# Neighbourhood attention: scores in three shared banks, division on the outputs, smaller weight buffers

## The chip, the cores and the metric

The kernel runs on one core of one Trainium2 chip. The metric is the device time of one execution in microseconds, taken as the median of several runs; lower is better. The profile comes from one further execution. The engines are TensorE (PE in the profile; PEld is its weight load), VectorE (DVE), ScalarE (ACT), GpSimd (POOL) and SyncE (SP), which issues nearly all DMAs of this kernel.

## The reference, cut to what matters

Two layers of a diffusion block work on 1024 latent tokens (a grid of 16 rows by 64 columns) and 256 context tokens, 1024 wide. Each layer modulates and normalises the tokens, multiplies them by one wide input matrix, gives its columns to four mixers (linear attention, neighbourhood attention, a state-space model, pooling), gates the four results, multiplies by an output matrix, normalises and adds. The neighbourhood attention, per head (4 heads of 64):

```
s_win = q @ k_rows + bias        # a window of 8 rows x 16 columns around the query; -inf outside
s_ctx = q @ k_context            # all 256 context tokens
p = softmax(concat([s_win, s_ctx], axis=-1), axis=-1)
o = p[window] @ v_rows + p[context] @ v_context
```

Context tokens attend to context tokens alone, without a bias. In the second layer they are no queries any more.

## The kernel before, in words

Every product that needs full accuracy is split: each operand is held as a rounded high half and a low half (float32r), and three products (high by high, high by low, low by high) are summed. `load_w` (L289) brings a weight matrix in pieces of `per` blocks of 128 rows: a raw piece by DMA, its high half by a cast on ScalarE (L301), its low half by a subtraction (L302). The pool `wp` has two raw buffers and three for each half (`WB`, L66), all as large as the largest piece: 1152 numbers, 4.5 KB a partition. Only the first projection of each layer, in `gla_proj` (L828), is 288 columns wide; the others are 128, 256 or 512 wide.

Attention (`na`, L1229) goes over jobs: a head and a block `qb` of 128 queries. Blocks 0 and 1 are the context (layer 0 only), blocks 2 to 9 cover 8 grid columns each. So a layer has 4 x 10 or 4 x 8 jobs, in rising order. An inner block meets 3 blocks of window keys and 2 of context (640 scores a query), the edge blocks 2 and 9 meet 2 and 2 (512), a context block 2 (256).

- `na_head` (L1267) loads what a head needs: the bias table of 1408 columns (one buffer; the inner table, the left and the right edge table, with zero columns for the context), negated on ScalarE (L1272), K (two buffers), Q in two tiles for blocks 0 to 4 and 5 to 9 (two buffers in all), V (one buffer). From block 6 on the next head's loads are asked for; those whose buffer is still in use wait on SyncE's queue.
- `na_scores` (L1291) multiplies Q by K into the tile `nS` (two banks of PSUM, one buffer), adds the bias on VectorE and takes the extreme of each row (L1321), forms the exponential and its row sum on ScalarE (L1326), takes the reciprocal (L1328) and multiplies the 640 probabilities by it (L1329).
- `na_turn` and `na_rest` turn the probabilities on TensorE (L1359) into `nT` tiles (one bank each, three buffers) three jobs later, and split them in halves (L1365 on ScalarE, L1366 on VectorE).
- `na_values` (L1369), two jobs later still, multiplies them by V for a pair of jobs (L1381), into the right half of the `nT` tile that `na_rest` used; ScalarE copies the lower partitions (L1383), VectorE adds the two parts into the head's output (L1395).

Pooling work on GpSimd and the first loads of the output stage (`out_early`) are woven in between. Beside the attention of layer 0, TensorE does five of the eight gate projections (`proj_gates`, L317), which have a later priority; in layer 1 they are done by 1155 us. The order on each engine's queue is fixed when the program is built: a planner takes the instructions by priority and by its own estimate of when each is ready. Every engine runs its queue in that order, SyncE its DMA issues too.

Of the kernel before, what the change touches and what calls it, by code (L numbers as in the profile page):

```python
# [12 lines left out]
F32 = mybir.dt.float32  # L13
F32R = mybir.dt.float32r
I32 = mybir.dt.int32
# [25 lines left out]
NRM = 0  # L41
# [19 lines left out]
NB = (1, 3)  # L61
# [9 lines left out]
class Kernel:  # L71
# [72 lines left out]
    def load_consts(self):  # L144
# [8 lines left out]
        self.sel = ld("sel", [128, 2])  # L153
        self.bmod = [c.tile([128, 24], F32, name=f"bmod{l}") for l in range(DEPTH)]
# [134 lines left out]
    def load_w(self, src, n, pool=(None, None), scale=None, engines=None, order=None):  # L289

        nc = self.nc
        per = min(8, 1152 // n)
        his, los = {}, {}
        for k0 in order or range(0, 8, per):
            hi, lo = (next(own, None) if own else None for own in pool)
            hi, lo = (w or self.t([128, per, n], "w" + x, b, self.wp, dtype=F32R) for w, x, b in zip((hi, lo), "hl", WB))
            raw = self.t([128, per, n], "w", WB[2], self.wp)
            (self.q(3) if order else self.q(4)).dma_start(raw, src[k0 * 128:(k0 + per) * 128, :].rearrange("(k p) f -> p k f", p=128))
# [677 lines left out]
    def gla(self, l, last):  # L976
# [6 lines left out]
        flag = self.const.tile([1, 1], I32, name=f"gflag{l}")  # L983
# [244 lines left out]

    def na(self, l, last):  # L1229


        with self.phase("na", True):
            pool = self.pooling(l, last)
            jobs = [(h, qb) for h in range(4) for qb in range(2 if last else 0, NT)]
# [6 lines left out]
            for i in range(len(jobs) + NALAG + 2):  # L1241
# [16 lines left out]
                if i < len(jobs):  # L1258
                    self.na_scores(l, live[i], last)
                if i == len(jobs) + OE:  # L1260
                    self.out_early(l, last)
# [5 lines left out]
    def na_head(self, l, h, last):  # L1267
        nc = self.nc
        rows = slice(64 * h, 64 * h + 64)
        bias = self.t([128, 1408], "nab", 1)  # L1270
        nc.sync.dma_start(bias, self.a["na_bias"][l, h])
        nc.scalar.activation(bias, bias, AF.Copy, scale=-1.0)  # L1272
# [16 lines left out]
        return h, K, Q, V, bias, self.na_y  # L1289

    def na_scores(self, l, job, last):  # L1291
# [3 lines left out]
        (h, K, Q, V, bias, yst), qb = job  # L1295
# [16 lines left out]
        for c, b, n in runs:  # L1312
            for i in range(2):
                nc.tensor.matmul(ps[:, c * 128:(c + n) * 128], lhsT=Qb[:, i, :], rhs=K[:, b * 128:(b + n) * 128],  # L1314
                                 start=(i == 0), stop=(i == 1))
        ps = ps[:, off * 128:off * 128 + nk]
# [3 lines left out]
        if blocks:  # L1320
            v.tensor_tensor_reduce(P[:, 0:nk], ps, bias[:, b0:b0 + nk], 1.0, -NEG, ALU.add, ALU.min, nm)  # L1321
# [30 lines left out]
    def na_psum(self, tag, n):  # L1352
        return self.ps2.tile([128, n], F32, tag=tag, bufs=NB[tag == "nT"], name=self.nm(tag))

# [14 lines left out]
    def na_values(self, l, job0, job1, last):  # L1369
        nc = self.nc  # L1370
        (h, K, Q, V, bias, yst), qb, r0, _, _, shared, PT, rest, ps = job0
# [39 lines left out]
    def pooling(self, l, last):  # L1411
# [3 lines left out]
        sc = self.t([128, 2], "psc", 1)  # L1415
        nc.sync.dma_start(sc, a["pool_sc"][l])
        wb = self.t([128, 2, 128], "pwb", 1)
# [307 lines left out]
```

## Time and profile before

| what | value |
|---|---|
| timed runs | 1373.57, 1375.45, 1379.98 us; median 1375.45 us |
| profiled execution | 1365.45 us; span of its instructions 1363.6 us |
| TensorE busy | 1244.4 us (91%), 7086 products |
| VectorE busy | 909.1 us (67%) |
| ScalarE busy | 584.0 us (43%) |
| GpSimd busy | 202.0 us (15%) |
| mean granted TensorE clock | 0.976 |
| attention of layer 0 | about 494 to 617 us of the span |
| attention of layer 1 | about 1155 to 1266 us |

A busy time counts an engine's instructions where they overlap once. TensorE's products are pipelined, so a run of them is shorter than the sum of their durations. A pause is put down to the instruction that ended it.

### The profile page before, as it was taken

The numbers are of one execution on the slowest core, as the hardware profiler recorded it, in microseconds if no ns is written. First come the engines' busy times: TensorE is split into PE (matmuls) and PEld (weight loads), VectorE is DVE, ScalarE is ACT, GpSimd is POOL, SyncE is SP. The second block draws the span as 40 slices with busy tenths as digits, with TensorE's granted clock in tenths as the row PEclk, the third lists the DMA queues.
The fourth block names the chain that finished last, engine by engine and source line by source line (L and its number), as shares of the span: only waits on it lengthen the run. The fifth ranks groups of instructions, "written<-read, shape, count | busy, mean of one in ns | idle before, by whom it ended". The sixth has DMA issues, their size and how long they took to land. (4 is left out here: it accounts for less than half of the span.)

```text
span 1363.6 us, 20304 instructions
## 1 busy us (share of the span) xinstructions
PE 1244.4 (91%) x7086; PEld 1001.4 (73%) x7086; DVE 909.1 (67%) x2269; ACT 584.0 (43%) x1218; POOL 202.0 (15%) x212
## 2 busy tenths in 40 slices
PE   5799999999999999979999999999999999777897
PEld 2698967677777688867778989768767776666676
DVE  2878587555387648873866788586644884786483
ACT  2652443223333347653555643443323333665321
POOL 0100000001100024351410000000111100235220
PEclk9898999999999999989999999999999999898999
DMA  9546596752533277747832475865216435764762
GB/s 320 183 132 215 196 261 175 229 158 78 167 122 122 72 198 196 221 138 220 257 111 93 126 226 193 256 187 157 85 53 197 160 108 163 204 168 127 209 205 88
DMA packets 231542, 231.08 MB, mean 169 GB/s; under 512 B 46888, under 2 KB 192808, under 8 KB 231104
## 3 DMA queue, kind: packets, MB, share of 16 engines
q1 hardware_dynamic: 229840, 227.14, 54.8%
q10 hardware_dynamic: 1584, 2.49, 0.5%
q8 instruction: 59, 0.97, 0.3%
q14 instruction: 59, 0.48, 0.1%
HBM read 159.97 MB, written 69.62 MB: 168 GB/s over the span
## 5 line engine op out<-in xcount | busy, mean ns | idle before, releaser
L317 PE MATMUL pa<-ahi,wh 128*128 128x512 f32 (+1 forms) x664 | 171.5, 386 | 3.7 <-DVE stg L346 1.5
L317 PE MATMUL pa<-ahi,wl 128*128 128x512 f32 (+1 forms) x664 | 167.2, 379 | 0.2 <-PEq L1554 0.2
L317 PE MATMUL pa<-alo,wh 128*128 128x512 f32 (+1 forms) x664 | 164.3, 377 | 0.4 <-PEq L1554 0.4
L317 PEld LDWEIGHTS pa<-ahi,wh 128*128 128x128 f32 x664 | 115.6, 192 | 29.0 <-issue 6.0
L317 PEld LDWEIGHTS pa<-alo,wh 128*128 128x128 f32 x664 | 116.0, 192 | 22.9 <-issue 4.8
L317 PEld LDWEIGHTS pa<-ahi,wl 128*128 128x128 f32 x664 | 115.5, 192 | 23.0 <-issue 5.6
L302 POOL TENSOR_TENSOR wl<-w,wh 128x1024 fp32r<-128x1024 f32 (+1 forms) x19 | 46.9, 2470 | 286.0 <-PE pa L317 153.2
L387 PE MATMUL po<-wx,ahi 128*128 128x512 f32 x312 | 79.9, 396 | 4.3 <-ACT ahi L379 2.5
L333 PE MATMUL pa<-wh,ahi 128*128 128x256 f32 (+1 forms) x480 | 78.4, 297 | 4.9 <-DVE ahi L260 2.3
L301 ACT CAST wh<-w 128x1024 fp32r<-128x1024 f32 (+1 forms) x51 | 53.8, 1056 | 59.1 <-PE pa L317 37.5
L333 PE MATMUL pa<-wl,ahi 128*128 128x256 f32 (+1 forms) x480 | 78.2, 296 | 0.1
L333 PE MATMUL pa<-wh,alo 128*128 128x256 f32 (+1 forms) x480 | 76.1, 293 | 0.0
L1314 PE MATMUL nS<-naK,naQ 128*128 128x256 f32 (+2 forms) x256 | 58.7, 348 | 17.4 <-DVE nast L1321 16.0
L333 PEld LDWEIGHTS pa<-wh,ahi 128*128 128x128 f32 x480 | 65.6, 191 | 10.0 <-issue 3.0
L387 PEld LDWEIGHTS po<-wx,ahi 128*128 128x128 f32 x312 | 59.2, 191 | 18.0 <-ACT ahi L379 3.5
L333 PEld LDWEIGHTS pa<-wl,ahi 128*128 128x128 f32 x480 | 66.4, 192 | 3.6 <-issue 2.5
L333 PEld LDWEIGHTS pa<-wh,alo 128*128 128x128 f32 x480 | 65.0, 190 | 3.3 <-issue 2.9
L1314 PEld LDWEIGHTS nS<-naK,naQ 128*128 128x128 f32 x256 | 43.5, 199 | 30.7 <-DVE nast L1321 26.0
L1321 DVE CUSTOM_DVE_ANT_0 naP<-nS,nab 128x640 f32<-128x640 f32 (+1 forms) x64 | 50.4, 787 | 17.6 <-ACT nab L1272 9.0
L1326 ACT ACTIVATE naP<-naP,nast 128x640 f32<-128x640 f32 (+1 forms) x64 | 51.6, 806 | 24.0 <-DVE nast L1321 21.2
L1381 PE MATMUL nT<-naPT,naV 128*128 128x256 f32 (+3 forms) x368 | 54.0, 286 | 7.4 <-DVE naPT L1366 5.4
L302 DVE TENSOR_TENSOR wl<-w,wh 128x1024 fp32r<-128x1024 f32 (+1 forms) x32 | 39.8, 1248 | 29.6 <-ACT wh L301 20.1
(395 smaller groups left out, 2561.7 us busy)
## 6 DMA issues: line engine op xcount, KB each, us to landing
w<-in_w_in_dram SPq DMA_DIRECT2D x41, 512.0 KB
wm<-in_w_mod_dram SPq DMA_DIRECT2D x32, 512.0 KB
s5R<-dR SPq DMA_DIRECT2D x16, 960.0 KB
xt<-in_tok_dram SPq DMA_DIRECT2D x20, 512.0 KB
wm<-in_w_mod_dram SPq DMA_DIRECT2D x8, 1024.0 KB
dR<-sp_R SPq DMA_DIRECT2D x16, 512.0 KB
dG<-stg SPq DMA_DIRECT2D x32, 256.0 KB
w<-in_w_out_dram SPq DMA_DIRECT2D x16, 512.0 KB
```

The costliest lines, as they stand in the source:

```text
L301: nc.scalar.copy(hi, raw)
L302: (next(engines) if engines else self.eng(2)).tensor_tensor(lo, raw, hi.bitcast(F32), ALU.subtract)
L317: nc.tensor.matmul(ps[:, :t1 - t0], lhsT=w(k), rhs=x[:, k, t0:t1], start=(i == 0), stop=(i == 23))
L333: nc.tensor.matmul(ps[:, :n], lhsT=x[:, k, t * 128:(t + 1) * 128], rhs=w(k), start=(i == 0), stop=(i == 23))
L387: self.nc.tensor.matmul(o, lhsT=x[:, k], rhs=m(k), start=first and i == 0, stop=last and i == len(todo) - 1)
L1314: nc.tensor.matmul(ps[:, c * 128:(c + n) * 128], lhsT=Qb[:, i, :], rhs=K[:, b * 128:(b + n) * 128], start=(i == 0), stop=(i == 1))
L1321: v.tensor_tensor_reduce(P[:, 0:nk], ps, bias[:, b0:b0 + nk], 1.0, -NEG, ALU.add, ALU.min, nm)
L1326: nc.scalar.activation(P[:, 0:nk], src, AF.Exp, bias=nm, scale=-1.0, accum_out=l1)
L1381: nc.tensor.matmul(out[:, q:q + n], lhsT=w, rhs=x, start=(i == 0), stop=(i == len(todo) - 1))
```

## The change

The scores' tile becomes one tile of 1536 columns (three banks) for the whole layer: even jobs write its columns 128 to 767, odd jobs 768 to 1407, so both use the middle bank. Blocks run in the order 0, 1 (layer 0), 4, 5, 2, 3, 6, 7, 8, 9. The bias table is one tile of 1792 columns: zeros, the inner table of even heads, zeros, the inner table of odd heads, zeros, and one place for an edge table that is refilled after block 2 (right edge) and after block 9 (left edge of the next head); each load is negated by itself. `NRM = 1` leaves the probabilities undivided: L1329 is gone, and in `na_values` TensorE turns the two reciprocal columns, broadcast to 64, into the left half of the products' bank, VectorE adds the two parts into `t` and multiplies by the turned reciprocals in a second step (these lines stood in the code before, unused). `load_w` cuts at 1024 numbers: the 288-wide matrix comes in pieces of 3, 3 and 2 blocks. Two small tiles are merged, and a flag is kept in one tile.

```diff
-NRM = 0
+NRM = 1
-NB = (1, 3)
     def load_w(...):
-        per = min(8, 1152 // n)
+        per = min(8, 1024 // n)
...
+            if k0 + per > 8:
+                hi, lo, raw = (x[:, :8 - k0] for x in (hi, lo, raw))
-            (...).dma_start(raw, src[k0 * 128:(k0 + per) * 128, :]...)
+            (...).dma_start(raw, src[k0 * 128:min(k0 + per, 8) * 128, :]...)
+    def na_bias(self, l, h, dst, src, n):
+        x = self.na_b[:, dst:dst + n]
+        self.nc.sync.dma_start(x, self.a["na_bias"][l, h, :, src:src + n])
+        self.nc.scalar.activation(x, x, AF.Copy, scale=-1.0)
     def na(self, l, last):
-            jobs = [(h, qb) for h in range(4) for qb in range(2 if last else 0, NT)]
+            order = ([] if last else [0, 1]) + [4, 5, 2, 3, 6, 7, 8, 9]
+            jobs = [(h, qb) for h in range(4) for qb in order]
+            self.na_b = self.t([128, 1792], "nab", 1)
+            for c0 in (0, 640, 1280):
+                nc.gpsimd.memset(self.na_b[:, c0:c0 + 256], 0.0)
+            self.na_bias(l, 0, 1536, 640, 256)
+            self.na_s = self.ps2.tile([128, 1536], F32, tag="nS", bufs=1, name=self.nm("nS"))
...
                     self.na_scores(l, live[i], last)
+                    if qb == 2:
+                        self.na_bias(l, h, 1536, 1152, 256)
+                    elif qb == 9 and h < 3:
+                        self.na_bias(l, h + 1, 1536, 640, 256)
     def na_head(self, l, h, last):
-        bias = self.t([128, 1408], "nab", 1)
-        nc.sync.dma_start(bias, self.a["na_bias"][l, h])
-        nc.scalar.activation(bias, bias, AF.Copy, scale=-1.0)
+        self.na_bias(l, h, 256 + 640 * (h % 2), 0, 384)
     def na_scores(self, l, job, last):
-        kb = [2 + b for b in blocks] + [0, 1] if len(blocks) != 2 else [0, 1] + [2 + b for b in blocks]
-        b0 = {0: 384, 7: 896}.get(j, 0)
+        odd = qb % 2
+        if len(blocks) == 3 and not odd:
+            kb, c0, b0 = [2 + b for b in blocks] + [0, 1], 1, 256 + 640 * (h % 2)
+        else:
+            kb, c0, b0 = [0, 1] + [2 + b for b in blocks], (6 if odd else 2 if blocks else 4), 640 * (h % 2) if len(blocks) == 3 else 1280
-        off = int(len(blocks) == 3)
-        for c, b in enumerate(kb, off):
+        for c, b in enumerate(kb, c0):
-        ps = self.na_psum("nS", 1024)
-                nc.tensor.matmul(ps[:, c * 128:(c + n) * 128], ...)
+                nc.tensor.matmul(self.na_s[:, c * 128:(c + n) * 128], ...)
-        ps = ps[:, off * 128:off * 128 + nk]
+        ps = self.na_s[:, c0 * 128:c0 * 128 + nk]
-            v.tensor_tensor_reduce(P[:, 0:nk], ps, bias[:, b0:b0 + nk], ...)
+            v.tensor_tensor_reduce(P[:, 0:nk], ps, self.na_b[:, b0:b0 + nk], ...)
```

## Rows read from the trace of the kernel before

**Rows 1.** Windows by stage: microseconds busy (instructions) of PE, PEld, DVE, ACT, POOL.

```profile
494.00:600.00 106.00, 102.47 (x667) 86.49 (x666) 90.12 (x226) 73.62 (x172) 45.93 (x60) 1.00 0.70 194
600.00:617.00 17.00, 11.18 (x51) 8.91 (x50) 7.09 (x16) 6.02 (x14) 9.70 (x11) 0.70 0.40 115
1155.00:1266.00 111.00, 81.45 (x491) 67.22 (x492) 80.83 (x200) 65.69 (x146) 41.16 (x56) 0.92 0.60 161
```

**Rows 2.** Windows of DVE alone: L1329 (first two rows), L1395 (last two).

```profile
494.00:617.00 123.00, 22.77 (x40) 0.96 0.66 183
1155.00:1266.00 111.00, 19.14 (x32) 0.92 0.60 161
...
494.00:617.00 123.00, 8.35 (x20) 0.96 0.66 183
1155.00:1266.00 111.00, 6.38 (x16) 0.92 0.60 161
```

**Rows 3.** DVE groups by form, 1155 to 1266: busy, mean ns | idle before, releaser.

```profile
L1321 DVE CUSTOM_DVE_ANT_0 naP<-nS,nab 128x640 f32<-128x640 f32 x24 | 19.7, 820 | 6.3 <-PE nS L1314 6.3
...
L1321 DVE CUSTOM_DVE_ANT_0 naP<-nS,nab 128x512 f32<-128x512 f32 x8 | 5.5, 690 | 6.8 <-ACT nab L1272 6.7
```

**Rows 4.** Chain of waits (start, duration); the second line from SyncE's timeline.

```profile
1151.03 3.77 DMA naQ<-dQ
...
1197.03 1.17 SPq L1283 DMA_DIRECT2D naQ<-dQ  x2
...
1174.18 4.84 DMA nab<-in_na_bias_dram
...
1199.22 4.98 DMA nab<-in_na_bias_dram
1204.23 1.39 ACT nab L1272
...
1271.78 4.46 DMA w<-in_w_out_dram
```

**Rows 5.** Timeline of PE: start, duration of the run, instruction, count.

```profile
1188.46 0.60 PE L1359 MATMUL nT<-c_ident,naP 128*128 128x128 f32 x4
...
1191.39 0.82 PE L1359 MATMUL nT<-c_ident,naP 128*128 128x128 f32 x6
...
1196.27 0.74 PE L1314 MATMUL nS<-naK,naQ 128*128 128x256 f32 x4 [0.38 <-DVE nast L1321]
...
1199.25 0.73 PE L1314 MATMUL nS<-naK,naQ 128*128 128x512 f32 x2
```

**Rows 6.** PE groups by form, 1155 to 1266.

```profile
L1359 PE MATMUL nT<-c_ident,naP 128*128 128x128 f32 x152 | 24.2, 291 | 3.3 <-DVE nay L1395 2.4 <-DVE naP L1329 0.9
L1314 PE MATMUL nS<-naK,naQ 128*128 128x384 f32 x48 | 16.9, 438 | 14.0 <-DVE nast L1321 14.0
```

**Rows 7.** Timelines of ACT, DVE and PE around the first projection of layer 1.

```profile
747.26 2.21 ACT L301 CAST wh<-w 128x1152 fp32r<-128x1152 f32 x2 [2.29 <-PE po L387]
...
748.46 2.63 DVE L302 TENSOR_TENSOR wl<-w,wh 128x1152 fp32r<-128x1152 f32 x2 [2.16 <-ACT wh L301]
...
749.23 1.30 PE L333 MATMUL pa<-wh,ahi 128*128 128x288 f32 x8
...
784.33 1.23 PE L333 MATMUL pa<-wh,alo 128*128 128x288 f32 x8
785.39 1.12 PE L317 MATMUL pa<-ahi,wh 128*128 128x256 f32 x8
```

**Rows 8.** Start: SyncE's and PE's timelines; GB/s moved in microseconds 20 to 60.

```profile
27.42 8.41 SPq L1493 DMA_DIRECT2D xt<-in_tok_dram  x8
36.90 5.26 SPq L298 DMA_DIRECT2D w<-in_w_in_dram  x2
...
40.03 1.94 PE L333 MATMUL pa<-wh,ahi 128*128 128x288 f32 x6 [2.28 <-DVE ahi L260]
...
GB/s 387 387 377 389 393 389 172 113 344 412 390 368 359 387 410 426 418 422 414 418 426 422 418 372 348 304 296 230 27 0 0 0 0 0 0 0 8 0 128 142
```

More of the change, by code (lines that the diff above doesn't have):

```diff
@@ L153, in load_consts @@
         self.sel = ld("sel", [128, 2])
+        self.gflag = c.tile([1, DEPTH], I32, name="gflag")
         self.bmod = [c.tile([128, 24], F32, name=f"bmod{l}") for l in range(DEPTH)]
@@ L297, in load_w @@
             raw = self.t([128, per, n], "w", WB[2], self.wp)
-            (self.q(3) if order else self.q(4)).dma_start(raw, src[k0 * 128:(k0 + per) * 128, :].rearrange("(k p) f -> p k f", p=128))
+            if k0 + per > 8:
+                hi, lo, raw = (x[:, :8 - k0] for x in (hi, lo, raw))
+            (self.q(3) if order else self.q(4)).dma_start(raw, src[k0 * 128:min(k0 + per, 8) * 128, :].rearrange("(k p) f -> p k f", p=128))
             if scale is not None:
@@ L982, in gla @@
         ch = lambda t: t.rearrange("p (c i) -> p c i", i=128)
-        flag = self.const.tile([1, 1], I32, name=f"gflag{l}")
+        flag = self.gflag[:, l:l + 1]
         with self.phase("glF", True):
@@ L1288, in na_head @@
             self.na_y = self.t([128, NTOK], "nay", 1)
-        return h, K, Q, V, bias, self.na_y
+        return h, K, Q, V, self.na_y
     def na_scores(self, l, job, last):
@@ L1294, in na_scores @@
         v = nc.vector
-        (h, K, Q, V, bias, yst), qb = job
+        (h, K, Q, V, yst), qb = job
         j = qb - 2
@@ L1310, in na_scores @@
                 runs.append([c, b, 1])
-        ps = self.na_psum("nS", 1024)
         for c, b, n in runs:
             for i in range(2):
-                nc.tensor.matmul(ps[:, c * 128:(c + n) * 128], lhsT=Qb[:, i, :], rhs=K[:, b * 128:(b + n) * 128],
+                nc.tensor.matmul(self.na_s[:, c * 128:(c + n) * 128], lhsT=Qb[:, i, :], rhs=K[:, b * 128:(b + n) * 128],
                                  start=(i == 0), stop=(i == 1))
-        ps = ps[:, off * 128:off * 128 + nk]
+        ps = self.na_s[:, c0 * 128:c0 * 128 + nk]
         P = self.t([128, 640], "naP", 3)
@@ L1320, in na_scores @@
         if blocks:
-            v.tensor_tensor_reduce(P[:, 0:nk], ps, bias[:, b0:b0 + nk], 1.0, -NEG, ALU.add, ALU.min, nm)
+            v.tensor_tensor_reduce(P[:, 0:nk], ps, self.na_b[:, b0:b0 + nk], 1.0, -NEG, ALU.add, ALU.min, nm)
             src = P[:, 0:nk]
@@ L1352, in na_psum @@
     def na_psum(self, tag, n):
-        return self.ps2.tile([128, n], F32, tag=tag, bufs=NB[tag == "nT"], name=self.nm(tag))
+        return self.ps2.tile([128, n], F32, tag=tag, bufs=3, name=self.nm(tag))
     def na_parts(self, PT, s0, ns, a0, a1, src):
@@ L1370, in na_values @@
         nc = self.nc
-        (h, K, Q, V, bias, yst), qb, r0, _, _, shared, PT, rest, ps = job0
+        (h, K, Q, V, yst), qb, r0, _, _, shared, PT, rest, ps = job0
         o = ps[:, 256:512]
@@ L1414, in pooling @@
         gp = nc.gpsimd
-        sc = self.t([128, 2], "psc", 1)
+        wb = self.t([128, 258], "pwb", 1)
+        wb, sc = wb[:, 0:256].rearrange("p (m n) -> p m n", m=2), wb[:, 256:258]
         nc.sync.dma_start(sc, a["pool_sc"][l])
-        wb = self.t([128, 2, 128], "pwb", 1)
         nc.sync.dma_start(wb, a["pool_wb"][l].rearrange("m k n -> k m n"))
```

1 line of the change is left out of this document (added).

## The prediction

> **What bounds the kernel now.** I read the stage table first, because this change touches two kinds of stage only: the attention stage of each layer (494 to 617 us and 1155 to 1266 us) and the first projection of each layer (34 to 101 us and 749 to 799 us). The attention of layer 0 runs beside gate projections that fill TensorE's pauses: TensorE is busy 102.47 of 106 us, VectorE 90.12 [rows 1]. The attention of layer 1 has hardly any filler left: TensorE 81.45 of 111 us, VectorE 80.83 [rows 1]. So layer 0 is near TensorE's limit and layer 1 is limited by something else, and the two answer differently to the same edit.
>
> For layer 1 I then read VectorE's groups and the chain of waits. Twice 6 to 7 us of VectorE's pauses stand ahead of the bias step L1321: 6.3 us until the scores came (640 columns wide) and 6.7 us until the negated bias table came (the 512-wide ones) [rows 3]. The second is the head boundary: the chain runs from the table's DMA (4.98 us) over its negation on ScalarE (1.39 us) to the first bias step of the next head [rows 4]. The tables of two following heads are loaded 25.0 us apart (1174.18 and 1199.22 us) [rows 4]; most of that time VectorE is the fullest engine. The reader is to see in rows 2 and 3 that in layer 1 a microsecond of VectorE is nearly a microsecond of the stage, and that a boundary costs VectorE 6.7/3 = 2.2 us, and about 1 us more until scores flow again (an estimate, from the 6.3 us of waits for scores over the same heads).
>
> **The division.** The step L1329 goes from all 72 jobs: 22.77 us of VectorE in layer 0 (40 jobs), 19.14 us in layer 1 (32 jobs) [rows 2]. In its place each of 36 pairs gets one more VectorE step of the form of L1395 (a sum first, then the multiplication): 8.35/20 = 0.42 us and 6.38/16 = 0.40 us each, so +8.35 us in layer 0 and +6.38 us in layer 1 [rows 2]. Net VectorE: -14.4 us and -12.8 us.
>
> It also adds 72 transposes of a broadcast column on TensorE. Four transposes take 0.60 us, six 0.82 us [rows 5]: one more in a row costs (0.82 - 0.60)/2 = 0.11 us, the first one 0.60 - 3 x 0.11 = 0.27 us. I take 0.11 us, as they come in pairs among other products: 40 x 0.11 = 4.4 us in layer 0, 3.5 us in layer 1; the upper end is 0.27 us each, 10.8 and 8.6 us. The Trainium skill has a price for this too (TensorE: Matmul & The Clock Gate, "Part 4: PE-mode transpose": about 275 ns for one in a kernel); rows 5 agree with it as a latency, not as a spacing.
>
> In layer 1 the 3.5 us fit into TensorE's 29 us of pauses, so they cost nothing by themselves; if that cover went they would cost the 3.5 us. They add a wait, though. The products' bank holds the sums beside the outputs; it is released only after copy, two transposes (0.27 + 0.11 us), sum and multiplication (0.40 us): 0.8 us later per pair. Queued behind that release are the next transposes of probabilities, which in layer 1 already wait 2.4 us for L1395 [rows 6], and behind them ScalarE's casts. Bounds: 0 (three buffers suffice) to 16 x 0.8 = 13 us; nearest row is the 2.4 us, so I take +2 us. The last pair of the stage adds its 0.8 us once at the end: +1 us.
>
> So for layer 1, of the 12.8 us of VectorE I count 0.8, a share that I choose because 80.83 of 111 us are busy and boundaries are counted apart: -10 us; bounds -5 to -12.8.
>
> **Scores in three banks.** Before, the next job's products wait until the whole tile is read: 14.0 us of TensorE's pauses in layer 1 stand ahead of the 384-wide products, all released by L1321 [rows 6]. After, even jobs use banks 0 and 1, odd jobs banks 1 and 2. The Trainium skill (PSUM — Partial Sum Buffer, "PSUM bank collisions raise a hardware error") says that an engine must be kept off a bank that another one reads, by bank and not by address; by that the pair of products in the middle bank still waits for the reader, and only the run in the outer bank goes ahead. Without that rule some 3 us more would go from VectorE's 6.3 us. No run shows yet which holds. I count nothing for the banks beyond the boundary's restart; bounds 0 to -6.3 us, of which the boundaries' restart already holds 3. The first edge block's two 512-wide products become four of 256: 0.74 against 0.73 us [rows 5], nothing.
>
> **Bias tables.** The inner table gets two places, so it is loaded a head ahead, and one edge place is refilled twice per head. The stalls at three boundaries in layer 1 go: -(2.2 + 1) x 3 = -9.7 us. What is late next is Q. The order is now 4, 5, 2, 3, 6, ..., 9, and the second Q tile (columns from 640) is read from job 5 on. Its buffer comes free with the scores of job 9 and it is needed by the second job of the next head (before: the fourth). Two issues take 1.17 us and the landing 3.77 us [rows 4]: 4.9 us, against one job of about 2.5 us. So up to 2.4 us per boundary; VectorE still has the lagging three jobs' work, so I take 0.9: +2.7 us. Queued behind these issues on SyncE are V, the edge table and the pooling inputs; the edge table (128 KB) has two jobs of lead, and I cost it at nothing, covered by them; uncovered it costs at most its negation and wait, 1 us a boundary. In layer 0 the two context jobs come first and cover Q. The three memsets on GpSimd and the merged tiles stand aside at nothing: GpSimd works 41 of 111 us [rows 1].
>
> Layer 1's attention: -10 - 9.7 + 2.7 + 2 + 1 = -14 us.
>
> **Layer 0's attention.** TensorE gets 4.4 us more, VectorE 14.4 us less, and the filler is conserved: what is not done beside attention is done after it. TensorE pauses only 3.5 us in 494 to 600 and 5.8 us in 600 to 617, the latter behind GpSimd's pooling [rows 1], which stays. I take 0 us: the freed VectorE lets small waits go that make up the 4.4 us. Bounds: -8 us (most of the 9.3 us of pauses and some waits inside the busy share) to +10.8 us.
>
> **Weights of 4 KB.** Only the 288-wide projection changes: three pieces (3, 3, 2 blocks) instead of two (4, 4). There are two raw buffers and three for each half.
> Layer 1: both raw pieces were long there when the casts ran at 747.26 us and the subtractions at 748.46 us [rows 7]. Now the third raw piece is issued only after the first subtraction: 2.63/2 x 864/1152 = 1.0 us after a cast of 0.83 us, so at about 749.2 us. Its 288 KB land after up to the 4.46 us of a 512 KB piece [rows 4], by size 2.5 us; with 0.4 us of issue and 0.6 us of cast it is ready at 752.7 us. TensorE wants it 6 x 0.13 us after 749.23 us [rows 7], at 750.0 us; the second tile's first six products fill 0.8 us. Cost 2 us (0 to 5).
> Layer 0: the third piece takes the slot at 36.90 us, behind eight token loads (4 MB) issued from 27.42 us on; the queues are empty by 48 us [rows 8]. TensorE went on at 40.03 us, so the piece can be up to 8 us late. Behind it on TensorE stand token transposes that wait for the same loads in any case, so I take 1 us (0 to 8).
> At the end of that projection all three buffers are now taken, so the next weight's cast waits for the last pass to be through its first three products, at 784.33 + 0.56 us (two spacings of 0.13 us and one product's 0.30). A 1024-wide cast takes 2.21/2 x 1024/1152 = 0.98 us, so it ends at 785.9 us, against a start at 785.39 us [rows 7]: 0.5 us and the signals between, 0.6 us, in both layers 1.2 us.
> Sum: +4 us (0 to 14).
>
> **Sum.** -14 + 0 + 4 = -10 us on the profiled execution's 1365.45 us, which gives 1355.5 us. That execution lay 10 us below the median of the timed runs (1375.45, from 1373.57 to 1379.98); the difference is carried over to the median: 1365.5 us. A measurement of this kernel can tell about 0.5%, 6.9 us, from no change.
>
> **Rivals.**
> Deeper gain: layer 0 takes VectorE's relief too (-8) and Q's wait is covered: -10 - 8 - 2.7, with less for the pieces: about 1353 us. For it: VectorE is busy 85% of 494 to 600 us. Against: TensorE at 97% there. Chance 0.13.
> No change: each turned sum costs its whole 0.27 us [rows 5]: +6.4 us more in layer 0, +8.6 us in layer 1, of which half finds no pause (4): -10 + 10 = 0, 1375 us. The Trainium skill's 275 ns (TensorE: Matmul & The Clock Gate, Part 4), counted as the price of each, gives the same. For it: layer 0's full TensorE; against: the spacing of 0.11 us. Chance 0.25.
> Slower: the products' bank, in every pair of both layers. The 0.8 us that it is held longer fall on TensorE, which runs in order: the two transposes wait for ScalarE's copy, and the next job's transposes for the release. If each pair pays 0.6 of these 0.8 us, 36 pairs cost 21.6 us, where I count 2; -10 + 19.6 = +9.6 us, 1385 us. It cancels the gain from 0.33 us a pair on and shows as slower from 0.53 us on. For it: TensorE already waits 2.4 us for L1395 there in layer 1 [rows 6]. [...] Against: three buffers, and in layer 0 filler products can stand in the gap. Chance 0.17.
> Forecast itself: 0.45.
>
> **Numbers.** Faster by over 0.5%: 0.45 + 0.13 = 0.58; within: 0.25; slower: 0.17. The bounds together would allow -33 us (layer 1 -12.8 - 9.7 - 3 + 1, layer 0 -8) to +34 us (layer 1 -5 - 9.7 + 7.2 + 3 + 13 + 1, layer 0 10.8, weights 14); leaving out one in ten at each end I take 1347 to 1382 us.
>
> **What would show it.** Right: L1329 gone and two steps per pair at L1395's place; no bias step behind a 1408-wide negation; in layer 1 attention about 97 us instead of 111, in layer 0 within 3 us of 123. Wrong: TensorE waiting for Q ahead of the second job of each head in layer 1 for more than 2 us; transposes of probabilities waiting for the last multiplication by far more than 2.4 us in sum; a pause of over 4 us after the first six products of either first projection.

## The result, and the profile after

The changed kernel takes 1386.29 us (median of 6 runs, 1382.23 to 1399.06), the kernel before 1376.21 us beside it (6 runs, 1371.58 to 1379.98). The ratio is 1.0091, 95% interval 1.0062 to 1.0120: 10 us slower by the medians and 12 us by the ratio, where 10 us faster was forecast, and above the range (1347 to 1382). The profiled execution took 1382.23 us (span 1380.4 us); the one of before lay 10 us under its median, so of differences between two profiles only those within a stage are used.

Windows of the changed kernel over the stages of [rows 1], with the same columns; each stage now starts 11 to 17 us later:

```profile
505.00:611.00 106.00, 99.58 (x654) 82.89 (x653) 72.75 (x198) 70.31 (x170) 42.24 (x59) 1.00 0.64 172
611.00:628.00 17.00, 12.72 (x76) 10.44 (x75) 8.02 (x20) 7.53 (x18) 8.94 (x12) 0.86 0.48 146
1172.00:1282.00 110.00, 93.74 (x600) 78.45 (x601) 73.50 (x187) 69.33 (x158) 40.47 (x56) 0.97 0.64 171
```

VectorE's relief came: 72.75 us busy where it was 90.12, and 73.50 where it was 80.83. By its own lines it is as large in layer 1 as was worked out: L1329's 19.14 us [rows 2] are gone, and L1411 and L1412 below take 13.2 us where L1395 took 6.7, so 12.6 us less; work of other stages fills a part of it. The stage of layer 1 is hardly shorter for it. TensorE is busier there (93.74 against 81.45 us), because 66 gate products that used to run ahead of the attention now run beside it, and the 32 turned sums are new.

VectorE's groups in 1172 to 1282, against [rows 3] (busy, mean ns | idle before, releaser); the last line is from before, 1155 to 1266:

```profile
L1340 DVE CUSTOM_DVE_ANT_0 naP<-nS,nab 128x640 f32<-128x640 f32 x24 | 19.6, 818 | 7.3 <-PE nS L1333 6.5 <-PE nT L1378 0.7
L1411 DVE TENSOR_TENSOR nat<-nT,nat 64x256 f32<-64x256 f32 x16 | 6.7, 417 | 12.5 <-PE nT L1410 9.2 <-ACT naPT L1384 2.1 <-PE nT L1378 0.9
L1412 DVE TENSOR_TENSOR nay<-nat,nT 64x256 f32<-64x256 f32 x16 | 6.5, 409 | 0.3
L1340 DVE CUSTOM_DVE_ANT_0 naP<-nS,nab 128x512 f32<-128x512 f32 x8 | 5.5, 685 | 1.7 <-PE nT L1378 1.6
...
L1395 DVE TENSOR_TENSOR nay<-nT,nat 64x256 f32<-64x256 f32 x16 | 6.7, 417 | 6.7 <-ACT nat L1383 6.3
```

The wait for the negated table (6.7 us) is gone. VectorE's wait ahead of the sum of the two parts grew: 12.5 us, 9.2 of them for the turned sums, where it was 6.7 us for ScalarE's copy. TensorE's groups there, against [rows 6]:

```profile
L1333 PE MATMUL nS<-naK,naQ 128*128 128x384 f32 x48 | 13.6, 366 | 2.5 <-DVE nast L1340 1.6 <-issue 0.9
L1400 PE MATMUL nT<-naPT,naV 128*128 128x256 f32 x64 | 15.0, 312 | 3.5 <-DMA naV<-dN 2.8 <-DVE naPT L1385 0.6
L1410 PE MATMUL nT<-c_ident,nast 128*64 128x128 f32 x32 | 7.0, 297 | 7.8 <-ACT nat L1402 7.4
```

The 14.0 us that TensorE waited for a free score tile are 2.5 us. New are the turned sums L1410, 0.22 us busy each and 7.4 us of waiting for ScalarE's copy, and 2.8 us until V landed.

The three banks did not do this. Bias steps of three jobs in a row and the score products between them, in the changed kernel (start, duration of the run, instruction, count):

```profile
1180.19 0.68 DVE L1340 CUSTOM_DVE_ANT_0 naP<-nS,nab 128x512 f32<-128x512 f32 x1
1180.94 0.85 PE L1333 MATMUL nS<-naK,naQ 128*128 128x256 f32 x4
1181.85 0.81 DVE L1340 CUSTOM_DVE_ANT_0 naP<-nS,nab 128x640 f32<-128x640 f32 x1
1182.72 0.85 PE L1333 MATMUL nS<-naK,naQ 128*128 128x384 f32 x4
1183.77 0.81 DVE L1340 CUSTOM_DVE_ANT_0 naP<-nS,nab 128x640 f32<-128x640 f32 x1
```

Each job's products start only when the bias step of the job before has ended, also where the first run goes to an outer bank that this step does not read (1182.72 us, 384 columns wide). 10 of the 24 jobs of both layers that begin with such a run start 0.06 us after it, and none of the 272 score products of this trace overlaps a step that reads the tile. So the whole tile is waited for, and whether a bank alone would do, which the prediction left open, stays open. The wait gets shorter without the banks too: with the division on the outputs alone, on the old tile, it is 5.5 us ahead of the 384-wide products and 2.5 us ahead of the 512-wide ones.

So VectorE's work in the attention moved as planned, and still the time went up. The stages say where. Each is taken from the starts of TensorE's first products of it (us, counted from 0.8 us into the span; the last column is the kernel below that has the division on the outputs in layer 1 alone, with two pieces, and the new tables and order in both layers):

| stage | before | changed | pieces in layer 0 only | pieces in layer 1 only | division in layer 1 alone |
|---|---|---|---|---|---|
| start to the first scores of layer 0 | 493.7 | 505.3 | 509.2 | 493.7 | 494.0 |
| attention of layer 0, to the first output product | 129.4 | 132.6 | 131.6 | 132.6 | 136.5 |
| from there to layer 1's first projection | 125.4 | 126.2 | 123.9 | 127.5 | 124.4 |
| first projection of layer 1 | 49.9 | 60.2 | 49.9 | 60.9 | 50.0 |
| from there to the first scores of layer 1 | 354.9 | 347.1 | 361.4 | 356.2 | 353.7 |
| attention of layer 1, to the last values | 111.1 | 108.1 | 112.6 | 113.6 | 105.2 |

The largest steps are 11.6 us ahead of layer 0's attention and 10.3 us in layer 1's first projection, of which 7.8 us come back. Neither stage holds any attention; both load the 288-wide weights. How far such a stage scatters between executions is seen over all kernels run here: the first row is 492.7 to 498.4 us in the nine that load layer 0's weights in two pieces, 505.3 to 516.5 in the nine that load them in three.

### The profile page after: what moved, and what is told of

Read it like the earlier page. It is cut to its first block, busy times and chain, and to the rows that moved or that the text cites. A ratio compares the mean times of both kernels' runs of the same rounds, so it can differ in the third digit from the quotient of the medians.

```text
span 1380.4 us, 20549 instructions
## 1 busy us (share of the span) xinstructions
PE 1256.4 (91%) x7174; PEld 1010.5 (73%) x7174; DVE 889.4 (64%) x2234; ACT 583.9 (42%) x1236; POOL 201.1 (15%) x219
## 5 line engine op out<-in xcount | busy, mean ns | idle before, releaser
L319 PE MATMUL pa<-alo,wh 128*128 128x512 f32 (+1 forms) x664 | 170.5, 385 | 0.0
L319 PE MATMUL pa<-ahi,wl 128*128 128x512 f32 (+1 forms) x664 | 161.5, 377 | 0.0
L304 POOL TENSOR_TENSOR wl<-w,wh 128x1024 fp32r<-128x1024 f32 (+2 forms) x20 | 47.3, 2369 | 299.4 <-PE pa L319 187.1
L335 PE MATMUL pa<-wh,ahi 128*128 128x256 f32 (+1 forms) x480 | 82.7, 302 | 5.9 <-DVE nr2w L137 2.2
L335 PE MATMUL pa<-wh,alo 128*128 128x256 f32 (+1 forms) x480 | 79.6, 298 | 0.0
L303 ACT CAST wh<-w 128x1024 fp32r<-128x1024 f32 (+2 forms) x53 | 54.2, 1026 | 55.2 <-PE pa L319 30.7
L304 DVE TENSOR_TENSOR wl<-w,wh 128x1024 fp32r<-128x1024 f32 (+2 forms) x33 | 39.5, 1208 | 46.7 <-ACT wh L303 37.8
L348 DVE SCALAR_TENSOR_TENSOR stg<-stg,pa 128x512 f32<-128x512 f32 (+1 forms) x40 | 25.1, 630 | 62.8 <-ACT stg L347 51.7
L1385 DVE TENSOR_TENSOR naPT<-nT,naPT 128x512 fp32r<-128x512 f32 (+1 forms) x104 | 56.9, 560 | 10.1 <-ACT naPT L1384 9.0
L974 POOL TENSOR_TENSOR qs<-QB,ind 128x512 f32<-128x512 f32 x18 | 19.1, 1060 | 277.7 <-PE pb L1063 164.8
```

The source lines that it names most:

```text
L319: nc.tensor.matmul(ps[:, :t1 - t0], lhsT=w(k), rhs=x[:, k, t0:t1], start=(i == 0), stop=(i == 23))
L335: nc.tensor.matmul(ps[:, :n], lhsT=x[:, k, t * 128:(t + 1) * 128], rhs=w(k), start=(i == 0), stop=(i == 23))
L348: nc.vector.scalar_tensor_tensor(th[:, :t1 - t0], th[:, :t1 - t0], 1.0, ps, op0=ALU.add, op1=ALU.mult)
L974: (nc.gpsimd if BD[d] == "p" else nc.vector).tensor_tensor(out, Q.unsqueeze(1).to_broadcast(sh), ind.unsqueeze(2).to_broadcast(sh), ALU.mult)
L1385: (nc.gpsimd if RLO == "p" and len(src) < 4 else nc.vector).tensor_tensor(lo, pv, hi.bitcast(F32), ALU.subtract)
```

## The experiments

Each is compared with runs of the kernel before on the same chip, so that two experiments are compared by their ratios. Ratios come with their 95% interval. "Pieces" are the 288-wide weights in 3, 3 and 2 blocks. Stage times are of one profiled execution each.

**Halves of the change.** Theory: the weights cost the time. Rival: the attention does (the turned sums and their waits).

Pieces alone, on the kernel before:

```
-        per = min(8, 1152 // n)
+        per = min(8, 1024 // n)
```

> The kernel before with one edit: weight pieces cut at 1024 numbers, so the 288-wide projection comes in three pieces (attention as before). Weights theory (the loss lies ahead of attention, in the three-piece projection of both layers and in what it delays): 10 to 17 us slower than before, with a pause of about 7 us on TensorE after the first six products of layer 1's first projection and attention's first scores of layer 0 some 10 us late. Attention theory (the loss comes from the new attention, the pieces cost the 4 us that were forecast): 2 to 5 us slower than before.

Measured 1391.85 us, 1.0127 [1.0092, 1.0161]: 17 us. The weights alone cost more than the whole change.

The changed kernel with two pieces again (its small statistics tiles packed into one, to make room):

```
-        per = min(8, 1024 // n)
+        per = min(8, 1152 // n)
```

> The changed kernel with two-piece weights again (1152 numbers); for the room the small statistics tile of attention is packed into one. Weights theory: 5 to 12 us faster than before, layer 1's attention shorter than before's 111 us and nothing late ahead of layer 0's attention. Attention theory: still 6 to 10 us slower than before.

Measured 1378.38 us, 1.0014 [0.9990, 1.0038]: neither theory's range. The new attention is worth nothing where -14 us was forecast.

The division on the outputs alone, on the kernel before:

```
-NRM = 0
+NRM = 1
```

> The kernel before with one edit: the division done on the outputs (NRM 1), old tables, order and scores tile. Weights theory: 3 to 8 us faster than before, from VectorE's relief in layer 1. Attention theory (the longer tail on the products' bank eats it): 0 to 10 us slower than before, with TensorE waiting over 7 us in layer 1 for ScalarE's copy ahead of the turned sums.

Measured 1377.77 us, 1.0016 [0.9992, 1.0039]: no change, so not the gain of the weights theory. The total lies in the attention theory's range, but its sign did not come: TensorE waits 3.1 us in layer 1 for the copy ahead of the turned sums, not over 7.

The changed kernel with the probabilities divided:

```
-NRM = 1
+NRM = 0
```

> The changed kernel with the division on the probabilities again (NRM 0), with its new tables, order, scores tile and three-piece weights. Weights theory: as slow as the changed kernel or slower (8 to 15 us over before), since the pieces stay and VectorE's relief is gone. Attention theory with the tail on the products' bank as cause: 3 to 10 us faster than the changed kernel, at before's time.

Measured 1390.60 us, 1.0121 [1.0092, 1.0149]: the weights' loss is there without the turned sums. With them, in the changed kernel, it was 1.0091; the intervals overlap.

**What in the pieces.** A third raw buffer, on the kernel before with pieces:

```
-WB = (3, 3, 2)
+WB = (3, 3, 3)
```

> The kernel before with the weights in pieces of 1024 elements (the 288-wide projection in three pieces of 3, 3 and 2 blocks) and a third raw buffer, so that no raw piece waits for a slot; the three buffers of each half are still all taken by that projection. Theory 'third raw piece' (it starts late because both raw slots are taken, and its cast and subtraction then stand behind other work on ScalarE and VectorE): the 17 us that the pieces alone cost shrink to 5 us or less, and the pause of about 9 us after the first six products of layer 1's first projection is gone. Rival 'all three halves taken' (the next weight's cast waits for the projection's end): still 10 to 18 us slower than before.

Measured 1387.07 us, 1.0079 [1.0054, 1.0104]: 11 us remain, and the pause of layer 1 with them (its first projection takes 60.3 us).

The changed kernel, the third raw piece in a buffer of its own:

```
-                hi, lo, raw = (x[:, :8 - k0] for x in (hi, lo, raw))
+                hi, lo = (x[:, :8 - k0] for x in (hi, lo))
+                raw = self.t([128, 8 - k0, n], "w2", 1, self.wp)
...
```

> The changed kernel, the third raw piece of the 288-wide projection in a buffer of its own (2.3 KB a partition). Theory 'third raw piece': 8 to 14 us faster than the changed kernel, so within 4 us of before, and layer 1's first projection starts as it does before. Rival 'all three halves taken': within 3 us of the changed kernel, 7 to 13 us slower than before.

Measured 1399.13 us, 1.0177 [1.0150, 1.0204]: not better but slower still. The raw piece's wait for a buffer is not the cause; why this kernel is slower than the changed one is open.

The traces show what holds the pause instead. ScalarE's timeline of the kernel with three raw buffers (start, duration of the run, instruction, count, idle before):

```profile
768.64 1.82 ACT L303 CAST wh<-w 128x864 fp32r<-128x864 f32 x2 [2.29 <-PE po L389]
778.60 0.67 ACT L303 CAST wh<-w 128x576 fp32r<-128x576 f32 x1
```

The third cast runs 10 us after the first two, with its raw piece long asked for (its DMA was issued at 703 us), because the written order has eight rows of token activations ahead of it. So it was raised in that order, in both kernels:

```
-            nc.scalar.copy(hi, raw)
...
+            with self.tc.high_priority() if k0 + per > 8 else ExitStack():
+                nc.scalar.copy(hi, raw)
...
```

> The kernel before with three weight pieces and three raw buffers, the third piece's cast and subtraction raised in the order of work, so that the cast follows the other two on ScalarE in place of standing eight rows later, behind the token activations. Theory 'third half buffer' (the third piece needs the half buffer that the output projection frees last, so its cast misses its turn on ScalarE by about 1 us and then stands behind 8 us of token work): the pause of 9 us at the start of layer 1's first projection shrinks to 3 us or less, total 4 to 8 us faster than without (which was 0.79% over before). Rival 'a few us everywhere' (the pieces lose time because all three halves are taken at the end of the projection too): the pause goes, but the total stays within 3 us of without.

> The changed kernel with the third raw piece in its own buffer, its cast and subtraction raised in the same way. Theory 'third half buffer': the pause shrinks from 9 to 3 us or less, total 4 to 10 us faster than without (which was 1.77% over before). Rival 'a few us everywhere': within 3 us of without.

The kernel with three raw buffers, third cast raised, ScalarE:

```profile
761.10 2.40 ACT L304 CAST wh<-w 128x864 fp32r<-128x864 f32 x3 [2.29 <-PE po L390]
```

All three casts run in a row, with no wait for a third half buffer. The stage shrinks from 60.3 to 53.8 us (54.8 in the other kernel), and the totals do not follow: 1391.96 us, 1.0108 [1.0072, 1.0143], and 1399.17 us, 1.0161 [1.0128, 1.0194]. So most of the pause was the cast's place in ScalarE's order, not the buffer that the theory named, and the pause is not the price. The traces show what takes the gain back: of the column products (the gate projections and their like, L317 in before), 41 ran beside layer 1's attention with the pause and 10 without (66 and 9 in the other kernel), and the stretch from that projection to the first scores of layer 1 grew from 348.8 to 358.7 us (349.1 to 357.5).

Then pieces in one layer only, buffers of the size of before:

```
         per = min(8, 1152 // n)
+        if n == 288:
+            self.w288 = getattr(self, 'w288', -1) + 1
+            if self.w288 == LP:     # 0 or 1
+                per = 3
```

> The kernel before with only layer 0's first projection loaded in three pieces (3, 3 and 2 blocks, in buffers of the size of before). Theory 'layer 0 pays' (all halves are taken at its first projection, so the next weight's cast moves from row 45 to row 73 of ScalarE's order and the VectorE-bound gate preparation behind it slips; 38 more filler products then stand ahead of layer 0's attention, which takes as long without them): 9 to 17 us slower than before. Rival 'layer 1's pause pays': within 4 us of before.

> The kernel before with only layer 1's first projection loaded in three pieces. Theory 'layer 0 pays': the pause of 9 us at its start is there, but the stages after it give back 6 us or more, so 0 to 5 us slower than before. Rival 'layer 1's pause pays': 8 to 14 us slower.

Measured: layer 0 alone 1392.11 us, 1.0112 [1.0081, 1.0143]; layer 1 alone 1382.82 us, 1.0052 [1.0028, 1.0075]. Layer 0's load carries most (15 us); layer 1's costs 7 us, 2 us more than its theory allowed. Added up they would be 22 us, where pieces in both layers cost 17.

**What ended layer 1's attention.** In the profile without pieces the scores ended 5 us earlier against their start, the last values did not. TensorE's timeline at the end of that stage, first before, then the changed attention without pieces:

```profile
1260.02 0.84 PE L1359 MATMUL nT<-c_ident,naP 128*128 128x128 f32 x5 [0.39 <-DVE naP L1329]
...
1263.62 0.70 PE L1459 MATMUL nT<-ps,pwb 128*128 128x256 f32 x2 [1.40 <-POOL ps L1450]
1263.97 1.48 PE L1381 MATMUL nT<-naPT,naV 128*128 128x256 f32 x10
```

```profile
1270.15 0.33 PE L1378 MATMUL nT<-c_ident,naP 128*128 128x128 f32 x1 [0.62 <-DVE naPT L1385]
...
1276.56 1.05 PE L1478 MATMUL nT<-ps,pwb 128*128 128x256 f32 x2 [2.93 <-POOL ps L1469]
1277.05 2.05 PE L1400 MATMUL nT<-naPT,naV 128*64 128x256 f32 x7
```

The last values stand on TensorE behind the last product of the pooling, and that product waits for GpSimd's last pooling step: it starts 3.6 us after the last transposes began in before, 6.4 us after in the other. The test advances the pooling one step every three jobs in place of four, in the changed kernel with the third raw piece's own buffer, and as a control in the kernel before (in both layers):

```
-PST = 4
+PST = 3
```

> As the kernel with the third piece's own buffer, and the pooling on GpSimd advanced one step every three attention jobs in place of every four. Theory 'pooling ends the stage' (layer 1's scores now end some 5 us earlier, but the last values stand on TensorE behind the last pooling product): 3 to 7 us faster than without it, layer 1's last values 3 to 6 us after the last transposes of probabilities no more. Rival 'V and the turned sums' (the attention waits inside, not at its end): within 2 us of it.

> Control: the kernel before with the pooling advanced every three jobs. Theory 'pooling ends the stage': here its last step ends with the last transposes of probabilities in any case, so the gain is 0 to 3 us, less than in the changed kernel. Rival 'V and the turned sums': within 2 us of before too; a gain as large as in the changed kernel would say that the pooling bounded both alike and did not swallow this change's gain.

Measured 1392.84 us, 1.0142 [1.0106, 1.0177], about 5 us under the same kernel without it (1.0177; the intervals overlap), layer 1's attention 102.3 us in place of 110.0. In the control 1380.86 us, 1.0038 [1.0018, 1.0058]: slower, where 0 to 3 us of gain were expected, and layer 1's attention is 113.0 us where it was 111.1. So the earlier pooling gives nothing to the attention of before.

The two-piece kernel with this in layer 1 only, and the same with the division on the outputs in layer 1 only:

```
-                if i % PST == PST - 1:
+                if i % (3 if last else PST) == (2 if last else PST - 1):
```

```
-        if NRM == 0:
+        if not last:
             v.reciprocal(r, l1)
...
-        if NRM:
+        if last:
             for i, r in enumerate((r0, job1[2])):
```

> The changed attention with the weights in two pieces as before, and the pooling advanced every three jobs in layer 1 alone (every four in layer 0). Theory 'pooling ends the stage': layer 1's attention, 111 us in before and without this edit, takes 101 to 105 us; total 5 to 9 us faster than without it, so 0.2 to 0.6% below before. Rival 'V and the turned sums' (V lands late at three heads and the sums are turned behind ScalarE's copy, whatever the pooling does): layer 1's attention 109 us or more, total within 2 us.

> As the last one, with the division done on the outputs in layer 1 alone; layer 0 divides the probabilities as before. Theory 'TensorE fills layer 0' (the 40 turned sums are 4 to 6 us more of TensorE's work there, and VectorE's relief buys nothing): layer 0's attention and the products after it 3 to 6 us shorter, total 3 to 6 us faster than the last one. Rival 'layer 0 takes the relief': within 2 us of it, or slower.

The first: 1375.73 us, 0.9997 [0.9978, 1.0016], layer 1's attention 105.4 us, near the 101 to 105 expected, the total 2 us under the kernel without it where 5 to 9 were expected. The second: 1368.43 us, 0.9940 [0.9920, 0.9959], 8 us below before: faster than both kernels, and 7 to 8 us faster than the first, where 3 to 6 were expected. End of layer 1's attention in the second, TensorE:

```profile
1261.08 0.33 PE L1378 MATMUL nT<-c_ident,naP 128*128 128x128 f32 x1 [0.34 <-DVE naPT L1385]
1263.53 1.29 PE L1400 MATMUL nT<-naPT,naV 128*128 128x256 f32 x10
```

No pooling product stands between them any more; 2.4 us separate them in place of 6.9.

Windows of layer 0's attention and the products after it, first with the division on the outputs in both layers, then in layer 1 alone:

```profile
492.00:627.00 135.00, 125.10 (x794) 104.19 (x793) 85.02 (x223) 81.99 (x193) 49.28 (x70) 0.99 0.60 163
```

```profile
494.00:627.00 133.00, 119.52 (x743) 100.81 (x742) 96.83 (x241) 80.61 (x192) 53.38 (x70) 0.96 0.61 165
```

In layer 0 that division costs TensorE 5.6 us of work (in a window 2 us longer) and saves VectorE 11.8. Of the 51 instructions more on TensorE 40 are turned sums; they take 8.3 us of its time there:

```profile
L1410 PE MATMUL nT<-c_ident,nast 128*64 128x128 f32 x40 | 8.3, 290 | 1.6 <-ACT nat L1402 0.9
```

TensorE is busy nine tenths of this stage either way. The stage itself is not shorter in the second profile (136.5 against 136.0 us), so in these two traces the turned sums are covered there; the totals differ by about 7 us, and their intervals don't meet. The stage behind it is where the profiles differ: from the first output product to layer 1's first projection 129.7 us with the division in layer 0, 124.4 without, the same 538 products at a granted clock of 0.96 and 0.99. But that stage took 125.3 us with the division on the outputs alone and 130.6 us in the control of the pooling, which divides the probabilities. So the total shows that this division costs time in layer 0; where it costs it isn't shown.

Last, the two halves of that kernel by themselves (the one with NRM = 0, the other the kernel before with the two edits above):

> The attention with three score banks, the new tables and the new order, the probabilities divided in both layers as before, two weight pieces, pooling advanced every three jobs in layer 1. Theory 'the division carries layer 1' (VectorE's 12.8 us are what the earlier pooling lets out): layer 1's attention 108 to 112 us, total at before's time, 5 to 9 us slower than with the division on the outputs in layer 1 (which was 0.6% below before). Rival 'banks and tables carry it': layer 1's attention 103 to 106 us, total within 3 us of that kernel.

> The counterpart: the kernel before with the division on the outputs in layer 1 alone and the pooling advanced every three jobs there; scores, tables, order and weights as before. Theory 'the division carries layer 1': layer 1's attention 103 to 107 us, total 4 to 9 us below before. Rival 'banks and tables carry it': layer 1's attention 109 us or more, total within 3 us of before.

Tables and order (and the three banks) without the division: 1370.64 us, 0.9959 [0.9941, 0.9976], layer 1's attention 109.1 us. The division in layer 1 without them: 1372.49 us, 0.9973 [0.9956, 0.9991], 107.5 us. Neither theory holds alone: each half gives 4 to 6 us, together 8, and with the division in layer 0 as well it is all gone (0.9997). On top of the tables and the order the division in layer 1 is worth 2.6 us of the total (0.9959 to 0.9940, intervals overlapping).

## Why the prediction was wrong

**Weights: +4 us forecast (0 to 14), 17 measured.** This is the step that failed first. For layer 0 it counted 1 us for the third piece and 0.6 for the next cast, for layer 1 2 us and 0.6. Layer 0's load alone costs 15 us.

The third piece itself did not come as assumed. SyncE's queue in the changed kernel, against [rows 8]:

```profile
26.99 1.40 SPq L1512 DMA_DIRECT2D xt<-in_tok_dram  x2
35.35 0.38 SPq L300 DMA_DIRECT2D w<-in_w_in_dram  x1
35.77 2.91 SPq L1512 DMA_DIRECT2D xt<-in_tok_dram  x6
```

The prediction put it behind eight token loads; it stands behind two and holds the other six until a raw buffer is free. That is not the price: with a third raw buffer the first scores of layer 0 came no earlier (516.5 us).

The next cast in layer 0, ScalarE and TensorE before, then changed:

```profile
59.81 1.04 ACT L301 CAST wh<-w 128x1024 fp32r<-128x1024 f32 x1
...
87.33 1.11 PE L317 MATMUL pa<-ahi,wh 128*128 128x256 f32 x8
```

```profile
87.58 2.00 ACT L303 CAST wh<-w 128x1024 fp32r<-128x1024 f32 x2
...
88.68 1.21 PE L319 MATMUL pa<-ahi,wh 128*128 128x256 f32 x8 [1.91 <-ACT wh L303]
```

Before, a spare half buffer let the next weight be cast 27 us ahead. With three pieces it is cast after the last product of the projection, and TensorE waits 1.9 us where 0.6 was counted. The wait is small; what follows isn't. The written order is another one, for TensorE already inside the first projection (before, it leaves the common order at 41.4 us) and for all that follows. VectorE's weight subtractions in 150 to 220 us before and 150 to 222 us changed:

```profile
L302 DVE TENSOR_TENSOR wl<-w,wh 128x1024 fp32r<-128x1024 f32 x5 | 6.1, 1220 | 4.5 <-ACT wh L301 3.8 <-PE pa L317 0.8
```

```profile
L304 DVE TENSOR_TENSOR wl<-w,wh 128x1024 fp32r<-128x1024 f32 x5 | 6.1, 1224 | 9.4 <-ACT wh L303 6.6 <-PE pa L319 2.8
```

VectorE stands idle 4.9 us longer ahead of the same five subtractions, in a stretch where it prepares layer 0's linear attention and was near its limit before (38 of 40 us busy from 180 to 220 us). And the filler, the column products of the gate projections, moved: counted in the two programs' order, 924 column products stand ahead of layer 0's first scores before, 955 after (962 with pieces in layer 0 only, 919 in the changed attention without pieces).

Over all kernels the loss has two places, and neither is the first projection. About 155 us into the span, at the first gate product of the linear attention (L900 in before), the nine kernels with three pieces in layer 0 are level with the nine with two (152.3 to 157.8 us against 153.1 to 157.5). From there to the product at L1009 they take 65.9 to 70.1 us against 61.1 to 63.8, and from the state-space model's first transposes (L729) to the first scores 138.6 to 143.0 us against 132.4 to 134.8. Windows of these two stretches, before and changed in turn:

```profile
153.91:214.96 61.05, 57.57 (x341) 47.13 (x339) 41.43 (x75) 30.20 (x43) 0.00 (x0) 1.00 0.81 235
152.31:218.51 66.20, 62.71 (x364) 51.16 (x363) 42.98 (x77) 31.31 (x45) 0.00 (x0) 1.00 0.76 225
360.70:494.48 133.78, 128.12 (x719) 98.19 (x718) 86.61 (x167) 49.00 (x101) 12.23 (x9) 1.00 0.42 134
364.06:505.98 141.92, 133.00 (x713) 100.50 (x713) 88.75 (x168) 48.55 (x102) 13.74 (x12) 0.96 0.40 127
```

TensorE's groups in the second stretch with the most idle time ahead of gate products, before and changed:

```profile
L317 PE MATMUL pa<-ahi,wh 128*128 128x512 f32 (+1 forms) x120 | 29.6, 370 | 1.5 <-DVE stg L346 1.5
L317 PE MATMUL pa<-alo,wh 128*128 128x512 f32 (+1 forms) x118 | 29.0, 368 | 0.4 <-PEq L1554 0.4
...
L319 PE MATMUL pa<-ahi,wh 128*128 128x512 f32 (+1 forms) x118 | 29.8, 376 | 5.1 <-PEq L1573 3.5 <-DVE stg L348 1.6
```

The first stretch is longer by TensorE's work, 5.1 us, with 21 column products more in it. The second has 5 column products fewer; TensorE is busy 4.9 us longer there at a lower granted clock, and idle 3.3 us longer, 3.1 of them at a conditional path of the program (L1554 in before, L1573 in the changed kernel; 1.8 to 3.7 us of idle time in the nine kernels, 0.2 to 0.4 in the others). So the moved filler accounts for some 5 of the 11.6 us.

The prediction held that filler is conserved, that what isn't done beside the attention is done after it. Done ahead of it, it isn't paid back: the attention of layer 0 took 129 to 133 us with it and without, and where it is gone TensorE pauses (15.9 of 131.6 us idle with pieces in layer 0 only, 9.1 of 129.4 before). Shown is which load costs the time, in which stretches, and that another order goes with it. Which link of the chain from the third piece and the late cast to the new order is the cause was not shown; a spare half buffer for three pieces didn't fit.

**Layer 1's pause.** The prediction named the sign: a pause of over 4 us after the first six products (of each of two tiles, as it came). It put it on the transfer. ScalarE and TensorE of the changed kernel, against [rows 7]:

```profile
762.83 1.83 ACT L303 CAST wh<-w 128x864 fp32r<-128x864 f32 x2 [2.29 <-PE po L389]
772.79 0.66 ACT L303 CAST wh<-w 128x576 fp32r<-128x576 f32 x1
...
764.79 1.87 PE L335 MATMUL pa<-wh,ahi 128*128 128x288 f32 x12
772.59 1.97 PE L273 MATMUL pb<-c_ident,stn 128*128 128x128 f32 x8 [3.86 <-ACT stn L484]
774.22 0.83 PE L335 MATMUL pa<-wh,ahi 128*128 128x288 f32 x2
```

The cast's place in ScalarE's order did most of it, as the raised cast showed. The pause has a second price. The whole stage, changed and then before (columns as in [rows 1]):

```profile
764.79:824.29 59.50, 52.39 (x336) 49.51 (x334) 39.69 (x140) 34.70 (x73) 0.10 (x1) 0.91 0.51 160
```

```profile
749.20:798.40 49.20, 48.63 (x336) 45.95 (x335) 35.78 (x124) 33.81 (x73) 0.10 (x1) 1.00 0.48 145
```

The same 336 products are busy 3.8 us longer, at a granted clock of 0.91 against 1.00: of 10.3 us, 6.5 are idle time and 3.8 go with the clock. It was 0.50, the lower level of 1.2 GHz, from 772.6 to 776 us, behind 3.9 us in which TensorE waited:

```profile
772.60:776.00 3.40, 3.40 (x15) 3.40 (x16) 3.40 (x8) 3.05 (x9) 0.00 (x0) 0.50 0.00 0
```

The Trainium skill (TensorE: Matmul & The Clock Gate, "Part 1: The HAM clock gate") has the array at half its clock by default and at full clock only with activity; the trace agrees. But most of the 10.3 us returned in the changed kernel: 61 column products fewer stand ahead of the same conditional path in layer 1 (1878 against 1939), and they ran in the pauses of its attention instead. Over the kernels it is less sure: the stretch from that projection to the first scores took 347.1 to 356.2 us in the seven that move 41 to 66 products into layer 1's attention, and 353.6 to 361.3 in the eleven others. Beside the attention filler costs little in either layer: layer 1's attention, as it was before, takes 113.5 to 114.8 us with 41 or 61 such products, and 111.1 (before), 112.6 (pieces in layer 0 only) and 114.0 us (raised cast) with 10 or none.

**Layer 1's attention: -14 us forecast, -3 measured (0 without pieces).** Its causes came: VectorE is relieved, the boundary's wait is gone, TensorE waits less for the score tile (the banks, counted at nothing, gave nothing). The step that failed is the one that let the stage's end follow VectorE. The pooling's end was in before's trace, 1.40 us of waiting for GpSimd in the stage's last products; all that the prediction said of GpSimd in layer 1 was that it works 41 of 111 us. With the pooling ahead the stage gives 5.9 us (105.2), still less than half of the 14. By the two halves, both with the pooling ahead, the division is worth 3.9 us of the stage (109.1 to 105.2; 3.6 on the kernel before) where 7 were counted (10 less 3 for its waits), and tables and order 2.0 (111.1 to 109.1; 2.3 the other way round) where 7 were too (9.7 less 2.7 for Q). The share of 0.8 of VectorE's relief was taken from its 80.83 us of 111; TensorE, at 81.45, was as full [rows 1].

**What came late next.** Not Q: in the changed kernel TensorE's waits for scores name VectorE alone, in layer 1 (in the kernel with tables and order without the division it waits 3.8 us for Q). V did: its one buffer is read until a head's last values and was needed one pair of jobs later, 2.8 us here and 6.3 us without the filler. The prediction listed V behind Q in SyncE's queue and gave it no price.

**The turned sums.** Held at 0.11 us each and covered in both layers. They are 0.2 us of TensorE each: 8.3 us for the 40 of layer 0, where 4.4 were counted. In layer 0 the division costs some 7 us of the total. The rival "no change" would explain it by these 8.3 us, but the stage of the attention is as long without them (136.5 against 136.0 us), so that this is the mechanism is not shown. The Trainium skill's 275 ns (TensorE: Matmul & The Clock Gate, "Part 4: PE-mode transpose") lies near the 282 to 297 ns of one here, and 0.2 us lies nearer to it than the spacing of 0.11 us that was taken. The "slower" rival, transposes of probabilities behind the products' bank, did not come: L1378 waits 1.2 us in layer 1 where L1359 waited 3.3 us [rows 6].

## What to carry to other kernels

An engine that is 40% busy can still set a stage's end, if its last step is queued ahead of the stage's last products: read the tail of the stage before counting a gain inside it. A load cut into more pieces moves no byte more, and yet it can rewrite an order of work that is computed from such times: compare the stretches that the edit does not touch, and count the filler ahead of each stage in both programs. A tile spread over more banks is worth something only if products run while the other part is read: look for one such product in the trace. And test an exchange of work between engines stage by stage: here the same division gains 2 to 4 us in layer 1 and costs 7 us in layer 0.

## What was not expected of the hardware

Runs of one kernel differ with the clock that they are granted: over 23 runs of before a mean granted clock lower by 0.01 went with 7 us more, and the kernel with pieces in layer 0 alone had 0.965 on the mean of its runs, the one with the division in layer 1 alone 0.975. So some 4 us of the pieces' price, an estimate by that slope against before's 0.970, go with a lower clock. Whether the clock is the cause there or follows from pauses that the pieces make isn't shown; the changed kernel had 0.970 on the mean of its runs, as before.
